# Strassen's scheme for four more K-tile pairs of a transformer block's products

## Chip, cores, metric

The kernel runs on one core of one Trainium2 chip. The metric is the device time of one launch in microseconds; lower is better.

## What is computed

One layer of a streaming encoder in float32, for 256 tokens of width 2048, with 256 memory tokens for the cross attention. All of the reference outside the four functions below only serves them (norms, rotary tables, masks, softmax):

```
h = LN(alpha*h + 0.5*SwiGLU_1(h))
h = LN(alpha*h + W_out[ sig(g_A)*(A(h) W_oA) + sig(g_B)*(B(h) W_oB) ])
      A = chunked attention with clipped relative-position bias
      B = multi-head latent attention, 16 heads of 128
h = LN(alpha*h + CrossAttn(h, LN(mem)))   (4 heads of 512)
h = LN(alpha*h + 0.5*SwiGLU_2(h))

def swiglu_ffn(x, w_in, w_out):
    g, u = jnp.split(x @ w_in, 2, axis=-1)      # x (256, 2048), w_in (2048, 2*5504)
    return (jax.nn.silu(g) * u) @ w_out
```

Three products matter here: the first SwiGLU's `x @ w_in`, the product with `w_o_b` (2048 x 2048) behind attention B, and the output projection `w_xo` (2048 x 2048) of the cross attention.

## The kernel before

**Products.** Each float32 value is split into a hi part (rounded to fp32r, by ScalarE, ACT) and a lo part (the rest, by VectorE, DVE), and a product is hi·hi + hi·lo + lo·hi, three matmul passes on TensorE (PE). The contraction runs over 16 K-tiles of 128 rows, taken in pairs, which are called steps or pairs here and numbered 0 to 7. An output group is 256 tokens (two token tiles) by two column blocks of up to 512, so four PSUM tiles. A plain pair (`mm_pair`, matmul at L300) is 2 K-tiles x 2 token tiles x 2 column blocks x 3 passes = 24 matmuls of up to 512 columns.

A Strassen pair (`mm_sums`, matmul at L354) treats the two K-tiles, two token tiles and two column blocks as a 2 x 2 product and does it with seven products (Winograd's form) instead of eight: 21 matmuls. It needs sums on both sides. Of the weights, one operation over 1024 columns (L190) and two over 512 (L192) on DVE make the summed blocks `t` in a tile called the stage; then ACT and DVE split them into hi (2 x 1024) and lo (2048). The raw weights that are split besides shrink from four blocks of 512 to three (1536). Of the activations, `sum_forms` (L306 to L323) makes four forms n5, s2, n3, s3 (one DVE operation of 512 at L310, four of 128 at L314), which are split into homes: half of a block tile, or four small `w1` tiles. Three of the seven products go to the group's own PSUM tiles `ps`, four to a second set `qs` (of the other PSUM pool); once the group's last Strassen pair is done, `shared` (L636 to L648) turns `qs` into four sums with two ACT copies and four DVE additions. Which pairs of a product are Strassen pairs is written in small tables at the top of the file (SUMS_IN, SUMS_YB, SUMS_XO), whose values are the homes of the forms. The weights are laid out for it ahead of the launch (`_pairs`).

**Order of work.** A list of items is built (`add`, `weave`), each with its weight loads, and `run` fetches raw weights through three `raw` tiles by SP's queue, splits them up to two units ahead, and emits the items. A scheduler then orders each engine's instructions by priority; the order below is what it yields. The hi tiles and the lo tiles have two buffers each.

**Places touched.** (1) The first FFN's first output group isn't in that list: `start` (L470) loads activations and weights pair by pair from the beginning of the program and does all eight pairs plainly, splitting weights in halves of 1024 (L236 lo, L235 hi). Its activations lie in blocks T0 to T3, two pairs each. After it, `ffn` (from L525) calls `hidden` for the group (SiLU times the up half) and makes the forms of pairs 2, 4 and 6 for the groups that follow. The second group's tiles are of the pool that `qs` of a first group would use. (2) Attention B's first output group, `out_b(0)` (L1140 on), uses Strassen for pairs 4 and 6; the forms are made at the end of the attention. The second group, `out_b(1)`, follows. (3) The cross attention's output (`cross`): its first two column groups go through `out_pair` with pairs 4 and 6 by Strassen, and the last head's softmax, transposition (L802) and product with the values (L1320) are woven into its first pairs; L1296 is the product of queries and keys.

## Time and profile before

| | us |
|---|---|
| median of 3 runs (2484.69 to 2485.30) | 2485.29 |
| the profiled execution | 2485.13 |
| its span in the trace | 2483.4 |
| PE busy | 2467.4 (99%) |
| DVE busy | 2066.2 (83%) |
| ACT busy | 1337.6 (54%) |

A row of the timeline gives the start in us from the span's beginning, the duration, engine, line, operation, output <- inputs, shape, and in brackets the idle time ahead of it and what ended it; rows of several instructions give the sum. In a row of the windows stand the stretch, its length, then for PE, PEld (weight loads), DVE, ACT and POOL the busy time and the number of instructions, the granted clock of PE (1.00 is full), the share of the DMA engines and GB/s. A row of PE's waits names the line that waited, the writer it waited for, the total, the count and the longest.

### The profile page before, as it was taken

To read this page: it belongs to the slowest core of one execution; us is meant where nothing else is said; L and a number is where in the kernel's file an instruction comes from. 1 tells how busy PE (TensorE), PEld (TensorE's weight loads), DVE (VectorE), ACT (ScalarE), POOL (GpSimd) and SP (SyncE) were. 2 spreads that over 40 slices of the span, in tenths; PEclk is the share of its full clock that TensorE was granted. 3 is DMA by queue.
4 is the path that set the end of the run, shared out by engine and by line. 5 is a ranking of instruction groups with operands and counts; after the bars stand their busy time and mean duration, and the time that the engine had idled before them with its cause. 6 is when DMAs were issued, how large, how long until landed. Compare 5 with 4: busy or idle time off the path is not lost.

```text
span 2483.4 us, 30482 instructions
## 1 busy us (share of the span) xinstructions
PE 2467.4 (99%) x11953; PEld 2079.9 (84%) x11953; DVE 2066.2 (83%) x2334; ACT 1337.6 (54%) x1803; POOL 31.8 (1%) x75
## 2 busy tenths in 40 slices
PE   9999999999999999999999999999999999999998
PEld 8888888889888888899888888888888888888886
DVE  6999889899778988677688798557888988898986
ACT  5555555555455555555455565545545555555552
POOL 0000000000000001000000000000000000000000
PEclk9999999999999999999999999999999999999999
DMA  7655556555645656554566547544655555655663
GB/s 259 240 196 204 187 200 211 203 187 204 237 155 210 212 203 219 178 163 141 172 235 217 189 174 248 189 155 150 209 197 187 203 187 204 210 198 202 203 216 140
DMA packets 72945, 490.16 MB, mean 197 GB/s; under 512 B 8449, under 2 KB 8961, under 8 KB 17633
## 3 DMA queue, kind: packets, MB, share of 16 engines
q1 hardware_dynamic: 67200, 468.29, 54.3%
q0 software_dynamic: 4448, 18.09, 2.2%
q8 instruction: 93, 1.52, 0.2%
q10 hardware_dynamic: 1152, 1.84, 0.2%
q14 instruction: 52, 0.42, 0.0%
HBM read 484.77 MB, written 2.10 MB: 196 GB/s over the span
## 4 chain that ended last, share of the span: by engine, by line
PE 93%; DVE 3%; DMA 2%; ACT 1%; issue 1%; DVEq 0%; ACTq 0%
PE mm L300 26%; PE at L300 24%; PE mm L354 10%; PE at L354 10%; PE mm L266 7%; PE mm L287 5%; PE mm L268 4%; PE mm L256 2%; DVE lo L246 1%; PE at L963 1%; DMA raw<-ffn_w_out_r 1%; PE at L802 1%; DMA raw<-w_xo_r 1%; PE at L1320 0%; PE at L405 0%
## 5 line engine op out<-in xcount | busy, mean ns | idle before, releaser
L243 ACT CAST hi<-raw 128x1024 fp32r<-128x1024 f32 (+1 forms) x848 | 800.9, 986 | 586.1 <-PE at L300 170.5
L246 DVE TENSOR_TENSOR lo<-raw,hi 128x2048 fp32r<-128x2048 f32 (+2 forms) x425 | 902.8, 2125 | 225.0 <-ACT hi L243 220.6
L300 PE MATMUL mm<-hi,T 128*128 128x512 f32 (+1 forms) x1280 | 298.2, 383 | 0.0
L243 ACT CAST X<-H 128x1024 fp32r<-128x1024 f32 (+1 forms) x162 | 165.0, 1034 | 220.4 <-DVE H L192 87.6
L300 PEld LDWEIGHTS mm<-hi,T 128*128 128x128 f32 x1280 | 238.3, 188 | 44.1 <-DVE H L833 0.3
L300 PE MATMUL at<-hi,T 128*128 128x512 f32 x1072 | 257.0, 389 | 0.0
L246 DVE TENSOR_TENSOR X<-H,X 128x2048 fp32r<-128x2048 f32 (+1 forms) x81 | 182.3, 2250 | 67.6 <-ACT X L243 67.6
L300 PEld LDWEIGHTS at<-hi,T 128*128 128x128 f32 x1072 | 201.1, 188 | 41.9
L300 PE MATMUL mm<-lo,T 128*128 128x512 f32 (+1 forms) x640 | 153.8, 382 | 0.0
L300 PE MATMUL at<-hi,H 128*128 128x512 f32 x592 | 140.7, 390 | 0.0
L300 PEld LDWEIGHTS mm<-lo,T 128*128 128x128 f32 x640 | 119.1, 188 | 21.8
L300 PE MATMUL at<-lo,T 128*128 128x512 f32 x536 | 132.6, 389 | 0.0
L300 PEld LDWEIGHTS at<-hi,H 128*128 128x128 f32 x592 | 110.9, 188 | 23.0 <-DVE w L647 0.2
L266 PE MATMUL mm<-T,hi 128*128 128x512 f32 x512 | 124.0, 393 | 0.0
L300 PEld LDWEIGHTS at<-lo,T 128*128 128x128 f32 x536 | 100.6, 188 | 20.9
L300 PE MATMUL mm<-hi,H 128*128 128x512 f32 x464 | 112.3, 392 | 0.0
L192 DVE TENSOR_TENSOR H<-H,raw 128x512 f32<-128x512 f32 (+1 forms) x162 | 109.3, 675 | 1.7
L266 PEld LDWEIGHTS mm<-T,hi 128*128 128x128 f32 x512 | 93.8, 188 | 19.3 <-issue 0.9
L300 PEld LDWEIGHTS mm<-hi,H 128*128 128x128 f32 x464 | 86.2, 188 | 17.6 <-DVE w L275 0.2
L190 DVE TENSOR_TENSOR H<-raw 128x1024 f32<-128x1024 f32 (+1 forms) x81 | 97.1, 1198 | 3.6 <-DMA raw<-ffn_w_in 2.4
L354 PE MATMUL mm<-X,X 128*128 128x512 f32 x348 | 95.7, 391 | 1.7 <-DVE H L236 1.7
L243 ACT CAST X<-raw 128x1024 fp32r<-128x1024 f32 (+1 forms) x54 | 55.3, 1036 | 52.1 <-DVE raw L192 31.5
(332 smaller groups left out, 3946.6 us busy)
## 6 DMA issues: line engine op xcount, KB each, us to landing
raw<-ffn_w_in SPq DMA_DIRECT2D x150, 1024.0 KB, 4.8
raw<-ffn_w_out SPq DMA_DIRECT2D x66, 1024.0 KB, 4.8
raw<-w_gate SPq DMA_DIRECT2D x32, 1024.0 KB, 4.9
raw<-ffn_w_out_r SPq DMA_DIRECT2D x16, 1024.0 KB, 4.9
raw<-w_qk SPq DMA_DIRECT2D x16, 1024.0 KB, 4.8
raw<-w_o_b SPq DMA_DIRECT2D x16, 1024.0 KB, 4.8
raw<-w_out SPq DMA_DIRECT2D x16, 1024.0 KB, 4.8
raw<-w_xk SPq DMA_DIRECT2D x16, 1024.0 KB, 5.0
```

Of the source, the lines that this page charges most:

```text
L190: self.nc.vector.tensor_tensor(two[0], two[1], raw[:, :m].unsqueeze(1).to_broadcast([P, 2, m]), ALU.add)
L192: self.nc.vector.tensor_tensor(t[:, a * m:a * m + m], t[:, b * m:b * m + m], raw[:, a * m:a * m + m], ALU.add)
L243: self.nc.scalar.copy(hi[:, c:d], src[:, c:d])
L246: self.nc.vector.tensor_tensor(lo[:, :n], src, hi[:, :n].bitcast(F32), ALU.subtract)
L256: self.nc.tensor.matmul(ps, w[wi][:, cols[j]:cols[j] + P], x.at(xi, kt), start=(j + wi + xi == 0), stop=(j == n - 1 and wi == 1),)
L266: self.nc.tensor.matmul(ps, hi[kt], x.both(kt), start=(kt == 0), stop=False)
L268: self.last_mm = self.nc.tensor.matmul(ps[:, :S], lo[kt], x.at(0, kt), start=False, stop=(kt == n - 1))
L287: self.last_mm = self.nc.tensor.matmul(ps, x.at(xi, kt)[:, tt * P:(tt + 1) * P], w[wi][:, j * 512 + c:j * 512 + c + m], start=(start and j ...
L300: self.last_mm = self.nc.tensor.matmul(ps[tt, g][:, :n], x.at(xi, kt)[:, tt * P:(tt + 1) * P], w[wi][:, c:c + n], start=first and j + wi + ...
L354: self.last_mm = self.nc.tensor.matmul(bank[:, :m], a[xi], v[wi][:, c * m:(c + 1) * m], start=own and first and wi + xi == 0, stop=own and ...
L802: self.nc.tensor.transpose(ps[:, i * P:(i + 1) * P], s[:, c:c + P], self.ident)
L963: nc.tensor.matmul(ps[:, c0:c0 + nk], q[:, tt * P:(tt + 1) * P], k[:, :nk], start=(j == 0), stop=(j == len(parts) - 1))
```

## The change

In `start`, pairs 4 and 6 go by Strassen (AT_FIRST). Their forms are made there, in the homes that the later groups use, and so no longer after `hidden`, where only pair 2's remain. The summed weights use the stage H5 and the blocks X2 and X3; `qs` comes from the pool `at`; `ffn` calls `shared` for the group ahead of `hidden`, which then takes its path with added sums. B's first output group gets pair 2 as a third Strassen pair (its forms in four `w1` tiles), and so do the cross output's first two column groups (its forms woven in at the second item). The second group of B stays as it is.

```
+AT_FIRST = 4, 6
-SUMS_YB = {4: ("T0", 0), 6: ("T0", 1)}
+SUMS_YB = {4: ("T0", 0), 6: ("T0", 1), 2: None}
+AT_YB = (2, 4, 6), (4, 6)
-SUMS_XO = {4: ("H2", 0), 6: ("H2", 1)}
+SUMS_XO = {2: None, 4: ("H2", 0), 6: ("H2", 1)}
...
+    def weight_sums(self, raw, m, t):
+        two = [v.rearrange("p (a m) -> p a m", a=2) for v in (t[:, :2 * m], raw[:, m:3 * m])]
+        self.nc.vector.tensor_tensor(two[0], two[1], raw[:, :m].unsqueeze(1).to_broadcast([P, 2, m]), ALU.add)
+        for a, b in ((2, 0), (3, 2)):
+            self.nc.vector.tensor_tensor(t[:, a * m:a * m + m], t[:, b * m:b * m + m],
+                                         raw[:, a * m:a * m + m], ALU.add)
+        return t
...
     def start(self):
...
+            if k in AT_FIRST:
+                if not qs:
+                    qs.update((a, self.group_tile(1)) for a in range(4))
+                self.forms_step(fx, SUMS_IN, k, lambda: xT, False)()
+                t4 = self.weight_sums(raw, 512, self.block("H5", (P, 2048)))
+                w = self.halves(raw[:, 512:], *self.unit()), self.halves(
+                    t4, *(self.block(g, (P, 2048), F32R) for g in SUM_HOME[0]))
+                self.mm_sums(ps, qs, w, 512, xT, fx[k], 2 * k, k == AT_FIRST[0], k == AT_FIRST[-1])
+                continue
             w = self.unit()
...
     def ffn(...)
                 if j == 0 and first is not None:
-                    main, ps = [], first
+                    main, (ps, qs, fx) = [], first
+                    self.add(lambda qs=qs: self.shared(qs, 512), prio=SOON)
...
-                    for c in SUMS_IN:
-                        self.add(self.forms_step(fx, SUMS_IN, c, xT))
+                    for c in set(SUMS_IN) - set(AT_FIRST):
+                        self.add(self.forms_step(fx, SUMS_IN, c, xT, False))
...
-            self.pair_group(g, t["w_o_b"][g], 512, KT, lambda: oB["t"], SUMS_YB, fb, ps, qs, None,
+            self.pair_group(g, t["w_o_b"][g], 512, KT, lambda: oB["t"], AT_YB[g], fb, ps, qs, None,
                             (("H5", "X2"), "X3"))
...
-        for c in SUMS_YB:
+        for c in (2, 4, 6):
             self.add(self.forms_step(fb, SUMS_YB, c, lambda: oB["t"]))
...
-        self.weave(self.collect(all_items), {2: last + [form(4)], 4: [form(6)]}, prio=0)
+        self.weave(self.collect(all_items), {1: [form(2)], 2: last + [form(4)], 4: [form(6)]}, prio=0)
```

The third argument `fresh=False` of `forms_step` lets the first form that is made, whichever it is, allocate the home's block. The weights' layout follows the tables. SP's and POOL's instructions stand in the same order as before, and PE has 12 matmuls fewer. In the changed file a line of before stands 4 lines lower up to `sum_forms` (L300 is L304, L354 is L358, L310 is L314, L246 is L250, L236 is L240) and 14 lower behind `start` (L1320 is L1334).

The scheduler's order changes in three regions, around the three places. In the start, DVE before has from pair 4 to pair 7 little but the lo parts of the weights (`lo`, in halves of 1024) and of the activations (`T`; `H_13` holds the raw activations):

```order
L236 TENSOR_TENSOR T_5_106<-H_13_126,T_5_106 128x2x256
L236 TENSOR_TENSOR lo_286<-raw_280,hi_285 128x1024 x2
L236 TENSOR_TENSOR T_6_107<-H_13_126,T_6_107 128x2x256 x2
L236 TENSOR_TENSOR lo_321<-raw_315,hi_320 128x1024 x2
L236 TENSOR_TENSOR lo_355<-raw_350,hi_354 128x1024 x2
L236 TENSOR_TENSOR lo_389<-raw_384,hi_388 128x1024 x2
L246 TENSOR_TENSOR lo_421<-raw_418,hi_420 128x2048
```

After the change it has, for pair 6 alone and what stands between (`H_49` is the stage, `w_48` the forms ahead of their split, `w_43` to `w_46` the split forms, `lo_432` belongs to pair 7, `X_53` is the lo part of the summed weights):

```order
L232 TENSOR_TENSOR H_49_392<-raw_369 128x1024
L318 TENSOR_TENSOR w_48_378<-w_47_377,w_48_378 128x128
L240 TENSOR_TENSOR w_43_373<-w_48_378,w_43_373 128x128
L240 TENSOR_TENSOR w_44_374<-w_48_378,w_44_374 128x128
L234 TENSOR_TENSOR H_49_392<-H_49_392,raw_369 128x512
L250 TENSOR_TENSOR lo_397<-raw_369,hi_396 128x1536
L240 TENSOR_TENSOR w_45_375<-w_48_378,w_45_375 128x128
L240 TENSOR_TENSOR w_46_376<-w_48_378,w_46_376 128x128
L234 TENSOR_TENSOR H_49_392<-H_49_392,raw_369 128x512
L240 TENSOR_TENSOR lo_432<-raw_427,hi_431 128x1024 x2
L250 TENSOR_TENSOR X_53_402<-H_49_392,X_52_401 128x2048
L250 TENSOR_TENSOR lo_464<-raw_461,hi_463 128x2048
```

One row of pair 6 has become the eleven ahead of the last, and the lo part of the summed weights has moved behind the lo part of pair 7. On PE, before, pair 6 is sixteen matmuls with hi and eight with lo on `T_6`, of which the first rows are:

```order
L300 MATMUL mm_121<-hi_354,T_6_107 128x512 x2
L300 MATMUL mm_122<-hi_354,T_6_107 128x512 x2
L300 MATMUL mm_123<-hi_354,T_6_107 128x512 x2
L300 MATMUL mm_124<-hi_354,T_6_107 128x512 x2
L300 MATMUL mm_121<-hi_354,T_6_107 128x512 x2
```

After, these are the last rows of pair 6 (`X_52` is the hi part of the summed weights, `at_285` to `at_288` are the tiles `qs`), with the beginning of pair 7 (`hi_431`) drawn in ahead of the products that read `X_53`:

```order
L358 MATMUL mm_122<-lo_397,w_45_375 128x512
L358 MATMUL at_285<-lo_397,T_6_107 128x512
L358 MATMUL at_286<-X_52_401,w_43_373 128x512 x2
L358 MATMUL at_288<-X_52_401,w_46_376 128x512 x2
L358 MATMUL at_287<-X_52_401,w_44_374 128x512 x2
L358 MATMUL mm_123<-X_52_401,T_6_107 128x512 x2
L304 MATMUL mm_121<-hi_431,T_6_107 128x512 x2
L304 MATMUL mm_122<-hi_431,T_6_107 128x512 x2
L358 MATMUL at_286<-X_53_402,w_43_373 128x512
L358 MATMUL at_288<-X_53_402,w_46_376 128x512
L358 MATMUL at_287<-X_53_402,w_44_374 128x512
L358 MATMUL mm_123<-X_53_402,T_6_107 128x512
```

Four matmuls of pair 7 have moved ahead of four of pair 6, which now wait for the last DVE row shown but one. At the cross output, DVE before (`lo_13462` is the lo part of pair 1, `w_2068` that of the last but one head's transposed probabilities, `sm_m` and `sm_r` the last head's softmax):

```order
L246 TENSOR_TENSOR lo_13462<-raw_13459,hi_13461 128x2048
L275 TENSOR_TENSOR w_2062_13454<-w_2062_13454,mm_13421 128x256
L236 TENSOR_TENSOR w_2068_13472<-at_13466,w_2067_13471 128x512
L790 TENSOR_REDUCE sm_m_13501<-at_13475 128x1 x2
L236 TENSOR_TENSOR H_2045_13285<-w_2062_13454,H_2045_13285 128x256
L791 TENSOR_SCALAR sm_m_13501<-sm_m_13501 128x2
L236 TENSOR_TENSOR H_2074_13516<-at_13517,H_2074_13516 128x256
L795 RECIPROCAL sm_r_13502<-sm_r_13502 128x2
```

and after (`T_2088` is the stage of pair 2's summed weights, `lo_13513` pair 1's lo part, `w_2091` the probabilities' lo part):

```order
L232 TENSOR_TENSOR T_2088_13519<-raw_13517 128x1024
L279 TENSOR_TENSOR w_2083_13505<-w_2083_13505,mm_13472 128x256
L250 TENSOR_TENSOR lo_13513<-raw_13510,hi_13512 128x2048
L804 TENSOR_REDUCE sm_m_13558<-at_13532 128x1 x2
L240 TENSOR_TENSOR H_2066_13336<-w_2083_13505,H_2066_13336 128x256
L805 TENSOR_SCALAR sm_m_13558<-sm_m_13558 128x2
L234 TENSOR_TENSOR T_2088_13519<-T_2088_13519,raw_13517 128x512
L240 TENSOR_TENSOR w_2091_13529<-at_13523,w_2090_13528 128x512
L234 TENSOR_TENSOR T_2088_13519<-T_2088_13519,raw_13517 128x512
L809 RECIPROCAL sm_r_13559<-sm_r_13559 128x2
```

The sums of pair 2's weights have moved up between the softmax's rows, and the lo part of the probabilities behind the softmax's maxima.

More of the change, by code (lines that the diff above doesn't have):

```diff
@@ L186, in form_sums @@
             if i < len(queue) and isinstance(queue[i], Sums) and i not in sums:
-                raw, m, home = fetch(i), queue[i].m, queue[i].stage
-                t = self.block(home, (P, 2048)) if home else self.raw_tile()
-                two = [v.rearrange("p (a m) -> p a m", a=2) for v in (t[:, :2 * m], raw[:, m:3 * m])]
-                self.nc.vector.tensor_tensor(two[0], two[1], raw[:, :m].unsqueeze(1).to_broadcast([P, 2, m]), ALU.add)
-                for a, b in ((2, 0), (3, 2)):
-                    self.nc.vector.tensor_tensor(t[:, a * m:a * m + m], t[:, b * m:b * m + m],
-                                                 raw[:, a * m:a * m + m], ALU.add)
-                sums[i] = t
+                raw, home = fetch(i), queue[i].stage
+                sums[i] = self.weight_sums(raw, queue[i].m, self.block(home, (P, 2048)) if home else self.raw_tile())
         def load(i):
@@ L328, in fn @@
                 tag, k = homes[c]
-                if k == 0:
+                if k == 0 and fresh or tag not in e:
                     e[tag] = self.block(tag, (P, 2, 2, 4, P), F32R)
```

10 lines of the change are left out of this document (5 added, 5 removed).

## The prediction

> **What bounds the kernel now.** I read the page first: busy times, then the granted clock.
>
> ```profile
> span 2483.4 us, 30482 instructions
> ...
> PE 2467.4 (99%) x11953; PEld 2079.9 (84%) x11953; DVE 2066.2 (83%) x2334; ACT 1337.6 (54%) x1803; POOL 31.8 (1%) x75
> ...
> PEclk9999999999999999999999999999999999999999
> ```
>
> TensorE (PE) works for 2467.4 of 2483.4 us at an undisturbed clock. So nothing but fewer or shorter matmuls can help much, and a wait of PE anywhere counts in full. VectorE (DVE), at 83%, is the only other engine near its limit. The profiled execution took 2485.13 us, 1.73 more than its span; the median of the runs shown is 2485.29. I add to 2485.13 and lift the result by 0.16 at the end.
>
> Next, the waits of PE, to see whether the engines that prepare its operands keep up:
>
> ```profile
> PE mm L354 <- DVE H L236: 1.7, 1, 1.7
> PE at L476 <- DVE w L452: 1.1, 1, 1.1
> PE at L802 <- DVE w L797: 0.6, 1, 0.6
> ```
>
> These are the three largest, and none is repeated. The kernel before feeds PE nearly without a gap.
>
> Then the chain of waits in order of time, for the price of a pair of K-tiles:
>
> ```profile
> 77.18 5.44 PE at L300 x24
> 87.38 5.44 PE at L300 x24
> ```
>
> A plain pair is 24 matmuls in 5.44 us, 0.2267 us each. Between the end of the first row (82.62) and the second (87.38) stands one Strassen pair: 4.76 us, just 21 × 0.2267. **A converted pair saves 0.68 us of PE**, if its operands come in time. The change converts four pairs: at most 2.72 us, 0.11% of the span. A measurement of this kernel can tell about 0.2% (5 us) from no change, so the size of the change sets the verdict; what remains is how much of the 2.72 survives in each place.
>
> What a Strassen pair costs is DVE work, so I need what DVE takes from one start to the next when nothing holds it:
>
> ```profile
> 16.70 1.22 DVE L236 TENSOR_TENSOR lo<-raw,hi 128x1024 fp32r<-128x1024 f32 x1
> 17.83 0.68 DVE L236 TENSOR_TENSOR T<-H,T 128x512 fp32r<-128x512 f32 x1
> ...
> 34.01 2.36 DVE L236 TENSOR_TENSOR lo<-raw,hi 128x1024 fp32r<-128x1024 f32 x2 [3.08 <-ACT hi L235]
> ...
> 48.52 1.42 DVE L192 TENSOR_TENSOR H<-H,raw 128x512 f32<-128x512 f32 x2
> ...
> 53.90 0.68 DVE L310 TENSOR_TENSOR w<-T 128x512 f32<-128x512 f32 x1
> 54.50 2.28 DVE L246 TENSOR_TENSOR X<-H,X 128x2048 fp32r<-128x2048 f32 x1
> 56.70 0.48 DVE L314 TENSOR_TENSOR w<-w 128x128 f32<-128x128 f32 x2
> ...
> 57.91 0.28 DVE L314 TENSOR_TENSOR w<-w,w 128x128 f32<-128x128 f32 x1
> 58.11 1.75 DVE L246 TENSOR_TENSOR lo<-raw,hi 128x1536 fp32r<-128x1536 f32 x1
> 59.78 0.68 DVE L236 TENSOR_TENSOR X<-w,X 128x512 fp32r<-128x512 f32 x1
> ```
>
> From start to start: 1024 wide 1.13 to 1.14, 512 wide 0.60, 2048 wide 2.20, 128 wide 0.20, 1536 wide 1.67. Each is some 0.08 below the recorded duration: the next operation starts before the record of the last ends. The row at 34.01 shows the slack before the change: in each step of the start DVE idles 3.08 us until ScalarE (ACT) has made the hi part.
>
> **The start (pairs 4 and 6 of the first group).** One row says how much room there is, and rows of PE when the room ends:
>
> ```profile
> 17.83:43.27 25.44, 25.44 (x113) 21.04 (x113) 14.39 (x15) 11.70 (x14) 0.00 (x0) 1.00 0.72 260
> ```
>
> ```profile
> 28.31 3.79 PE L300 MATMUL mm<-hi,T 128*128 128x512 f32 x16
> ...
> 50.07 3.79 PE L300 MATMUL at<-hi,T 128*128 128x512 f32 x16
> ```
>
> Pair 4 begins at 28.31 and the second group at 50.07. If PE never waited after the change, pair 4 would take 4.76 and pair 5 5.44. In the order of after, 17 matmuls of pair 6 follow (3.85) and the first four of pair 7 (0.91). Then PE wants the lo part of pair 6's summed weights, the last operand of a Strassen pair: at 28.31 + 4.76 + 5.44 + 3.85 + 0.91 = 43.27. DVE's order puts 35 operations between 17.83 and that point, where the row of the windows has 15: eight of 1024, eleven of 512, two of 1536, two of 2048 and twelve of 128. That is 8 × 1.14 + 11 × 0.60 + 2 × 1.67 + 2 × 2.20 + 12 × 0.20 = 25.86 us. **25.86 us of work stand in a gap of 25.44**: the idle time is used up. To this I add the waits inside: two operations need the result of the one ahead (0.11 each; in the row at 48.52 the second of two such operations ends after 1.42 where 0.60 + 0.68 = 1.28 would be without, so 0.14 at most), and DVE hands pair 6's forms to ACT for a cast and takes them back, 0.52 in all by my walk down the queues. ACT casts of 512 and less take up to 0.6 us (below, 1701.58), so this wait lies between nothing and 0.6. The lo part is then done at 17.84 + 25.86 + 0.74 = 44.44, and with 0.17 to reach PE (an estimate; the record's end alone is 0.08 behind the next start) its matmuls start at 44.61, not 43.27. Of this 1.34, 0.36 falls earlier: the lo of one form stands behind a 1536-wide operation on DVE and holds PE within pair 6. After 44.61 come 24 matmuls (5.44), and the second group begins at 50.05, against 50.07. **Term: 0.** The 1.36 saved is paid back in waits. Its ends: −1.36 if DVE is 1.3 us earlier, and +2.8 if each operation holds DVE for its recorded time (35 × 0.08). I take the middle because the quoted starts are unambiguous.
>
> The other new work of this group is covered. Adding up the products (two ACT copies, four DVE additions) frees the PSUM banks that the second group writes first: by the walk at 49.3 where PE wants them at 51.0. The forms that the first group now makes early are no longer made after it. The weight loads keep their order on SP's queue; with the page's 4.8 us for each they land, by the walk, at least 1.7 us before ACT needs them (pair 7 and the second group's first two are the late ones).
>
> ```profile
> raw<-ffn_w_in SPq DMA_DIRECT2D x150, 1024.0 KB, 4.8
> ```
>
> **B's first output group.** Here DVE has room.
>
> ```profile
> 1232.30 2.29 DVE L246 TENSOR_TENSOR lo<-raw,hi 128x2048 fp32r<-128x2048 f32 x1 [1.66 <-ACT hi L243]
> ```
>
> ```profile
> 1237.32 3.79 PE L300 MATMUL mm<-hi,T 128*128 128x512 f32 x16
> ```
>
> ```profile
> 1226.44:1280.00 53.56, 53.56 (x240) 44.38 (x239) 43.03 (x37) 24.55 (x27) 0.05 (x1) 1.00 0.54 189
> ```
>
> Pair 2 begins at 1237.32. Its operands need 1.14 + 2 × 0.60 (sums), 1.67 and 2.20 (two lo parts), 6.21 us, instead of 2.20: 4.0 more. The lo part of the row at 1232.30 waits 1.66 on ACT, and 10.5 us of DVE's 53.56 are idle in the stage. The walk has the first lo part ready at 1234.7 (wanted 1238.7) and the second at 1233 or shortly after (wanted 1241.2). The forms, 0.60 + 4 × 0.20 + 4 × 0.20, are made in the last attention steps, where DVE waits for ACT. **Term: −0.68**, with an end of 0 if the 4 us collide with `done` and its four multiplications; margins of 3 us and more speak against this.
>
> **The cross output.**
>
> ```profile
> 1677.34:1715.33 37.99, 37.99 (x230) 33.55 (x229) 30.77 (x54) 19.33 (x40) 0.00 (x0) 1.00 0.32 114
> ```
>
> ```profile
> 1680.64 3.22 PE L1320 MATMUL at<-w,H 128*128 128x256 f32 x24
> ```
>
> ```profile
> 1677.69 2.29 DVE L246 TENSOR_TENSOR lo<-raw,hi 128x2048 fp32r<-128x2048 f32 x1 [2.04 <-ACT hi L243]
> ...
> 1680.23 0.69 DVE L236 TENSOR_TENSOR w<-at,w 128x512 fp32r<-128x512 f32 x1
> ```
>
> ```profile
> 1699.32 2.00 ACT L243 CAST hi<-raw 128x1024 fp32r<-128x1024 f32 x2 [3.44 <-PE mm L300]
> 1701.58 0.59 ACT L235 CAST w<-at 128x512 fp32r<-128x512 f32 x1 [0.25 <-PE at L802]
> ```
>
> DVE is busy 30.77 of 37.99; the new 4.0 us and 2.2 of forms fit in the 7.2 idle us, barely. The 1024-wide sum falls into the 2.04 us of idle time ahead of the row at 1677.69. Behind it the softmax's operations and a 512-wide sum stand ahead of the lo part of the transposed probabilities (1680.23 in before): it is ready at 1683.5. PE has 13 of the first pair's matmuls (2.95) woven into the 24 that start at 1680.64, and wants it at 1683.84. A margin of 0.3. Later the cast of the last head's probabilities (before: 1701.58, in an idle ACT) stands behind the second half of a 2048-wide cast. One 1024 takes 1.0 of the 2.00 there, and that bounds the wait: 0 to 1.0. The walk gives 0.3, part of which the next matmuls would have spent anyway. **Term: −0.5**, ends −0.68 and +0.3.
>
> **Sum:** 0 − 0.68 − 0.5 = −1.2, so 2483.9 beside the profiled execution and 2484.1 beside the median; I say 2484.0. If every pair paid in full it would be 2482.4.
>
> **A rule against the change.** The rows 53.90 and 54.50 show the next DVE operation starting 0.08 before the last one's record ends. The Trainium skill, "VectorE: DVE Perf Modes", section "The DRAIN you can't avoid", says that the next operation waits until the pipeline of the last is empty. By that rule each of the start's operations would hold the engine for its whole record, and the time would be that of the second rival below; these two rows of the trace do not agree with it.
>
> **The rivals.**
> 1. *The start hides its DVE work* (chance 0.12). The lo part of pair 6 comes by 43.2. For it: ACT's hand-over may overlap with other operations, and the row at 34.01 shows 3.08 idle each step. Against it: the sum is 25.86 in 25.44 before any wait. All four pairs then pay: 2482.4.
> 2. *Slower: the start's DVE queue overruns* (0.13). The operations hold DVE for their recorded 0.28, 0.68, 1.22, 1.75 and 2.29, so 28.7 instead of 25.86 us. Pair 6's lo part is done at 47.2, the second group begins 2.8 late, and 2.8 − 0.68 − 0.5 = +1.6 gives 2486.7. It decides from 45.6 on, 1.2 us past my walk. Against it stand the starts quoted above; for it, that several of the 35 wait for results of the operation ahead or of ACT.
> 3. *The cross output gives its gain back* (0.12): the sums of weights ahead of the softmax delay the probabilities by more than the margin of 0.3, and PE waits 0.7 to 1.5: 2484.3 to 2485.1.
> 4. *The change does not do what it says* (0.03): PE's list still has all matmuls, 2485.1. The order shows 12 fewer, so only through a fault in reading it.
>
> **How the numbers follow.** My forecast (2483.3 to 2484.8) has 0.57, the rivals 0.12, 0.13, 0.12 and 0.03, and 0.03 is left for what I have not seen. The range reaches from 2482.2 (the first rival) to 2486.7: it takes in the first, third and fourth rivals and half of the second, and leaves out some 0.1. Faster by over 0.2% means below 2480.3, which no sum here reaches, 2482.4 being the floor: 0.02. Slower by over 0.2% means above 2490.3, more than twice the overrun: 0.04. The rest, 0.94, is within 0.2%.
>
> **What would show it.** PE's count falls by 12 matmuls, its busy time by 2.7. In the start, PE waits once for a DVE lo part just after the first four matmuls of pair 7 (near 43.3 to 44.6) and the second group begins near 50.05; 48.7 there is the first rival, 52 or more the second. B's first group: a pair of 4.76 at 1237 with no wait. Cross output: the pair after the third begins near 1714.8 on the scale of before plus what came earlier. The prediction is wrong if DVE's starts in the start stretch by more than 0.03 each, or if a load arrives late in the first 45 us, where the row of the windows shows the DMA queues at 0.72 and 260 GB/s.

## The result, and the profile after

The changed kernel takes **2481.99 us** (median of 22 runs, 2480.99 to 2483.89); the kernel before took 2485.61 beside it (22 runs, 2483.86 to 2488.49). The ratio is 0.9984, with a 95% interval of 0.9978 to 0.9989: some 3.6 us are gone, where 1.2 were forecast. The two profiled spans differ by 3.1 (2483.4 and 2480.3), and it is these two traces that can be compared place by place.

The page of the profile after, busy times and clock; line numbers of the helpers are 4 higher than before, those behind the start 14 higher:

```profile
span 2480.3 us, 30522 instructions
...
PE 2464.6 (99%) x11941; PEld 2076.9 (84%) x11941; DVE 2091.1 (84%) x2374; ACT 1347.4 (54%) x1821; POOL 31.8 (1%) x75
...
PEclk9999999999999999999999999999999999999999
```

PE has 12 matmuls fewer and is busy 2.8 us less: the change does what it says. The other 0.3 of the 3.1 is a balance of waits, and the list of PE's waits shows that they have changed place:

```profile
PE at L480 <- DVE w L456: 1.1, 1, 1.1
PE at L919 <- DVE X L925: 0.9, 1, 0.9
PE at L358 <- DVE X L250: 0.8, 1, 0.8
PE at L816 <- DVE w L811: 0.8, 1, 0.8
PE at L409 <- DVE h L401: 0.2, 1, 0.2
```

The largest wait of before, 1.7 at the Strassen products (L354, now L358, `mm`), is gone. Two are new. The one at L358, `at`, is the start's, which was forecast. The one at L919 stands in attention A, where the change edits nothing, and was not.

To see what each place gained I cut each trace at the same points of the program and took the time between PE's starts there (us):

| stage | before | after | difference |
|---|---|---|---|
| span's start to pair 1 of the start | 11.99 | 11.64 | −0.35 |
| **pair 1 to the second group (the start)** | 38.08 | 37.87 | −0.21 |
| second group | 42.59 | 42.41 | −0.18 |
| attention A to B's first group | 278.71 | 279.99 | **+1.28** |
| **B's first group and the next, to the transposes** | 53.04 | 52.36 | −0.68 |
| **cross output, to its pair 4** | 37.99 | 37.03 | −0.96 |
| second FFN's first Strassen pair on, one group | 44.40 | 42.70 | **−1.70** |
| from there to the end | 600.23 | 599.81 | −0.42 |

Each of the three stretches left out differs by 0.1 at most. The three places that the change edits, with the second group, give 2.0 of the 3.1. The stages in which it edits nothing give the rest: −0.35 + 1.28 − 1.70 − 0.42 = −1.2.

The rows of the start that answer to those of the prediction. PE first, from pair 4 to the second group:

```profile
27.96 0.62 PE L358 MATMUL mm<-hi,T 128*128 128x512 f32 x2
...
42.03 1.07 PE L304 MATMUL mm<-hi,T 128*128 128x512 f32 x4
43.94 0.96 PE L358 MATMUL at<-X,w 128*128 128x512 f32 x3 [0.83 <-DVE X L250]
44.74 0.39 PE L358 MATMUL mm<-X,T 128*128 128x512 f32 x1
44.97 2.89 PE L304 MATMUL mm<-hi,T 128*128 128x512 f32 x12
```

The wait stands exactly where the prediction put it, behind the first four matmuls of pair 7, and it is for the lo part of pair 6's summed weights. By the starts PE is 1.00 late there: it wanted the operand at 42.03 + 0.91 = 42.94 and began at 43.94 (the 0.83 in brackets counts from the end of the last record). The 24 matmuls behind it take 5.57 instead of 5.44. So the start loses 1.15 of its 1.36, where the prediction had 1.34. DVE says why: some of its rows of the stretch, and the row of the windows over all of it.

```profile
17.67 0.68 DVE L240 TENSOR_TENSOR T<-H,T 128x512 fp32r<-128x512 f32 x1
18.39 0.69 DVE L314 TENSOR_TENSOR w<-T 128x512 f32<-128x512 f32 x1
...
35.44 0.28 DVE L318 TENSOR_TENSOR w<-w,w 128x128 f32<-128x128 f32 x1
35.64 0.48 DVE L240 TENSOR_TENSOR w<-w,w 128x128 fp32r<-128x128 f32 x2
...
41.59 2.28 DVE L250 TENSOR_TENSOR X<-H,X 128x2048 fp32r<-128x2048 f32 x1
```

```profile
17.83:43.94 26.11, 26.04 (x36) 1.00 0.69 255
```

DVE is busy 26.04 of 26.11 us. From 17.67 to the start of the last row it takes 23.92, where the walk had 24.41. The 0.49 between them is nearly the hand-over to ACT, 0.52 in the walk: the rows at 35.44 and 35.64 follow each other without a gap, so other operations cover it. From the start of the operation behind the lo part (43.80) it takes PE 0.14 to begin; the estimate was 0.17.

In B's first group pair 2 takes 4.76, with no wait:

```profile
1237.95 0.62 PE L358 MATMUL mm<-hi,T 128*128 128x512 f32 x2
1238.40 0.62 PE L358 MATMUL mm<-hi,w 128*128 128x512 f32 x2
...
1242.71 1.52 PE L304 MATMUL mm<-hi,T 128*128 128x512 f32 x6
```

At the cross output, PE ahead of and behind the last but one head's products with the probabilities (L1320, now L1334):

```profile
1680.70 0.40 PE L1334 MATMUL at<-w,H 128*128 128x256 f32 x2
1680.94 3.14 PE L304 MATMUL mm<-hi,H 128*128 128x512 f32 x13
1683.91 2.80 PE L1334 MATMUL at<-w,H 128*128 128x256 f32 x22
1686.55 0.60 PE L816 MATMUL at<-ident,w 128*128 128x128 f32 x4
1686.90 3.12 PE L1310 MATMUL at<-X,H 128*128 128x256 f32 x24
```

and the same in before:

```profile
1683.70 0.40 PE L300 MATMUL mm<-hi,H 128*128 128x512 f32 x1
1683.94 0.68 PE L802 MATMUL at<-ident,w 128*128 128x128 f32 x4
1684.40 3.14 PE L1296 MATMUL at<-X,H 128*128 128x256 f32 x24
1687.38 3.04 PE L1320 MATMUL at<-w,H 128*128 128x256 f32 x24
1690.26 3.59 PE L300 MATMUL mm<-hi,H 128*128 128x512 f32 x15
```

In before, the 24 matmuls that began at 1680.64 (a row of the prediction) lasted until 1683.70, 3.06 us; the next 24 of the same kind take 2.88 (1687.38 to 1690.26). So 0.18 was lost there. The four transposes took 0.46 (1683.94 to 1684.40), after 0.35 (1686.55 to 1686.90), so 0.11 more was lost. After, 13 matmuls of pair 0 stand ahead of most of these products, and both losses are gone: 0.29, where the stage gained 0.28 beyond 0.68. The records of the single instructions of before fit: the third of the 24 products begins at 1680.97, just behind the end of the probabilities' lo part (1680.92), and the second transpose at 1684.07, just behind the end of the softmax's division (L797, 1684.01).

### The profile page after: what moved, and what is told of

Same layout as the page of the kernel before. It is cut to its first block, busy times and chain, and to the rows that moved or that the text cites. A ratio compares the mean times of both kernels' runs of the same rounds, so it can differ in the third digit from the quotient of the medians.

```text
span 2480.3 us, 30522 instructions
## 1 busy us (share of the span) xinstructions
PE 2464.6 (99%) x11941; PEld 2076.9 (84%) x11941; DVE 2091.1 (84%) x2374; ACT 1347.4 (54%) x1821; POOL 31.8 (1%) x75
## 4 chain that ended last, share of the span: by engine, by line
PE 95%; DVE 3%; DMA 1%; issue 0%; ACT 0%; SPq 0%; DVEq 0%; ACTq 0%
PE at L304 25%; PE mm L304 24%; PE mm L358 10%; PE at L358 10%; PE mm L291 7%; PE mm L270 7%; PE mm L272 4%; PE mm L260 2%; PE at L977 1%; PE at L291 1%; PE at L816 1%; DMA raw<-ffn_w_in 1%; PE at L1334 0%; PE at L1310 0%; PE at L1018 0%
## 5 line engine op out<-in xcount | busy, mean ns | idle before, releaser
L250 DVE TENSOR_TENSOR lo<-raw,hi 128x2048 fp32r<-128x2048 f32 (+1 forms) x427 | 905.8, 2122 | 206.7 <-ACT hi L247 204.9
L304 PE MATMUL mm<-hi,T 128*128 128x512 f32 (+1 forms) x1232 | 287.4, 382 | 0.0
L304 PEld LDWEIGHTS mm<-hi,T 128*128 128x128 f32 x1232 | 228.8, 188 | 42.9 <-ACT hi L239 0.8
L304 PE MATMUL at<-hi,T 128*128 128x512 f32 x1072 | 257.2, 389 | 0.0
L250 DVE TENSOR_TENSOR X<-H,X 128x2048 fp32r<-128x2048 f32 (+1 forms) x83 | 186.9, 2252 | 67.1 <-ACT X L247 66.0
L304 PEld LDWEIGHTS at<-hi,T 128*128 128x128 f32 x1072 | 201.1, 188 | 41.9
L304 PE MATMUL mm<-lo,T 128*128 128x512 f32 (+1 forms) x616 | 147.9, 382 | 0.0
L304 PE MATMUL at<-hi,H 128*128 128x512 f32 x592 | 140.9, 390 | 0.0
L304 PE MATMUL at<-lo,T 128*128 128x512 f32 x536 | 132.4, 389 | 0.0
L304 PEld LDWEIGHTS mm<-lo,T 128*128 128x128 f32 x616 | 114.6, 188 | 20.9
L304 PEld LDWEIGHTS at<-hi,H 128*128 128x128 f32 x592 | 110.9, 188 | 23.3 <-DVE w L661 0.4
L304 PEld LDWEIGHTS at<-lo,T 128*128 128x128 f32 x536 | 100.6, 188 | 20.9
L304 PE MATMUL mm<-hi,H 128*128 128x512 f32 x448 | 108.2, 392 | 0.0
L304 PEld LDWEIGHTS mm<-hi,H 128*128 128x128 f32 x448 | 83.4, 188 | 17.2 <-DVE w L279 0.2
L358 PE MATMUL mm<-X,X 128*128 128x512 f32 x348 | 95.7, 391 | 0.0
L358 PE MATMUL at<-X,X 128*128 128x512 f32 (+1 forms) x315 | 83.8, 384 | 0.0
```

Of the source, the lines that this page charges most:

```text
L250: self.nc.vector.tensor_tensor(lo[:, :n], src, hi[:, :n].bitcast(F32), ALU.subtract)
L304: self.last_mm = self.nc.tensor.matmul(ps[tt, g][:, :n], x.at(xi, kt)[:, tt * P:(tt + 1) * P], w[wi][:, c:c + n], start=first and j + wi + ...
L358: self.last_mm = self.nc.tensor.matmul(bank[:, :m], a[xi], v[wi][:, c * m:(c + 1) * m], start=own and first and wi + xi == 0, stop=own and ...
```

## The experiments

"Undone" means that the tables at the head of the kernel are set back. The changes in stages named below are from each run's own trace.

### Each part alone, and none

Theory 1 says that each place pays what its stage shows; theory 2 that the change shifts later loads for good, so that what was gained elsewhere comes with any part. The four kernels undo all but one part, or all three:

```
AT_FIRST = ()               # start undone, and the added `shared` under `if AT_FIRST:`
AT_YB = (4, 6), (4, 6)      # B undone, and its forms made in a loop over (4, 6)
SUMS_XO = {4: ...}          # cross output undone, and `1: [form(2)]` out of the weave
```

Only the start:

> Only the start goes by Strassen (pairs 4 and 6 of the first group); B and the cross output as before. Theory 1 (each place pays what its stage shows in the two traces): the second group begins 37.9 us after pair 1's first matmul instead of 38.1, the following group loses its 0.36 wait, so -0.4 to -0.6 us in all, with one PE wait of 0.8 to 1.0 on the lo part of pair 6's summed weights. Theory 2 (the start pays in full over many runs, the profile was unlucky): -1.3 us and no such wait. On record before: 0.

Only B's first group:

> Only B's first output group has the third Strassen pair. Both theories: pair 2 takes 4.76 instead of 5.44 us of PE with no wait beside it, -0.68 us. The stage from pair 0 of this group to the next group: 42.16 before, 41.48 here.

Only the cross output:

> Only the cross output has the third Strassen pair. Theory 1: the stage from the transposition ahead of the first pair to pair 4 takes 37.03 us as in the trace of the change, 37.99 before: -0.96, which is 0.28 more than 21 matmuls for 24; nothing else changes beyond chance. Theory 2 (the change shifts the weight loads that follow, and so takes away the 1.69 us wait at the second FFN's first Strassen pair for good): -2.6 us, that wait gone. The prediction on record: -0.5.

All undone, as a control:

> All three edits undone in the changed file (the program of before). A control: 0 us. Theory 1 (chance): of the waits of 0.9 to 1.7 us in the two traces that the edits do not touch (second FFN's first Strassen pair, attention A's key transposition, last column group), some are here, some not. Theory 2: the 1.69 us wait at the second FFN is here again.

| | median | ratio to before, interval | start | B | cross | second FFN's group | attention A |
|---|---|---|---|---|---|---|---|
| only start | 2483.92 | 0.9994, 0.9985 to 1.0003 | 37.26 | 53.05 | 37.99 | 42.71 | 279.56 |
| only B | 2484.33 | 0.9995, 0.9986 to 1.0004 | 38.08 | 52.37 | 37.99 | 44.29 | 278.67 |
| only cross | 2483.55 | 0.9993, 0.9984 to 1.0002 | 38.08 | 53.05 | 37.04 | 42.65 | 278.42 |
| none | 2485.05 | 0.9998, 0.9989 to 1.0007 | 38.08 | 53.04 | 37.99 | 43.60 | 278.60 |

(11 runs each; before in this comparison 2485.48, 33 runs.) The intervals are as wide as the parts, so the medians alone settle nothing; the stages do. B is worth −0.68 and the cross output −0.95, in each trace in which they stand, and nothing where they don't. So theory 1 holds at these two. The start is worth more alone (−0.82) than in the whole change (−0.21). And the last two columns move without an edit there: theory 1 has no account of them. Against the second theory in its plain form, the second FFN's group differs between before (44.40) and the control (43.60), which run the same work.

PE's rows of the start alone tell why the start's gain is not fixed:

```profile
43.98 0.97 PE L358 MATMUL at<-X,w 128*128 128x512 f32 x3 [0.25 <-DVE X L250]
44.78 0.39 PE L358 MATMUL mm<-X,T 128*128 128x512 f32 x1
45.01 2.89 PE L304 MATMUL mm<-hi,T 128*128 128x512 f32 x12
47.74 1.98 PE L304 MATMUL mm<-lo,T 128*128 128x512 f32 x8
49.55 2.65 PE L304 MATMUL at<-hi,T 128*128 128x512 f32 x11
```

Here PE began pair 1 at 12.29, 0.65 later than in the whole change (11.64), and yet the lo part is used at the same time (43.98 and 43.94) and the second group begins at the same time (49.55 and 49.51). **Before, PE paced the start** (38.08 in every trace without the edit, wherever it began); **now DVE does.** In the four traces with both pairs and this order, DVE takes 23.91 to 23.93 from the row that stands at 17.67 in after to the start of that lo part, wherever PE began. What PE saves is eaten by a wait when PE begins early, and kept when it begins late. When it begins is chance: the five traces that have the start of before and 12 warm-up matmuls have pair 1 at 11.54 to 12.26.

### What moved in the stages that nothing edits

The second FFN's first Strassen pair waited 1.69 in before. DVE began its sums late, since a 1 MB load had not landed:

```profile
1829.27 1.23 DVE L190 TENSOR_TENSOR H<-raw 128x1024 f32<-128x1024 f32 x1 [2.42 <-DMA raw<-ffn_w_in]
```

After, the same operation waits less:

```profile
1826.59 1.23 DVE L232 TENSOR_TENSOR H<-raw 128x1024 f32<-128x1024 f32 x1 [1.38 <-DMA raw<-ffn_w_in]
```

The DMA rows give that load's time: before (issued in the window 1823.2 to 1823.4), the control (1822.2 to 1823.0), and after (1821.6 to 1821.9).

```profile
raw<-ffn_w_in SPq DMA_DIRECT2D x1, 1024.0 KB, 6.0
```

```profile
raw<-ffn_w_in SPq DMA_DIRECT2D x1, 1024.0 KB, 5.9
```

```profile
raw<-ffn_w_in SPq DMA_DIRECT2D x1, 1024.0 KB, 4.9
```

What lies beside it? In before, in the window 1826.3 to 1826.5, the page's otherwise idle queue q8 moves one packet of 0.02 MB:

```profile
q8 instruction: 1, 0.02, 29.7%
```

After, its packet at this place comes in 1825.6 to 1825.9, behind the issue by 4.16 instead of 3.19:

```profile
q8 instruction: 1, 0.02, 18.5%
```

The page has the whole queue:

```profile
q8 instruction: 93, 1.52, 0.2%
```

93 packets of 16 KB for some 23,900 instructions of PE (matmuls and weight loads) are one for each 256; that they fetch PE's instructions is worked out from this count and from the queue's name. **Theory F**: such a fetch, when it falls into the first 3.7 us of a 1 MB load, delays it by about 1 us. An edit that takes out PE instructions moves all later fetches against the loads. **Theory C**: what differs in the unedited stages is chance from run to run. Since the number of PE instructions ahead of a place sets which one brings the fetch, the length of the warm-up (matmuls that compute nothing) is a handle that edits nothing else:

```
- WARM = 12
+ WARM = 8          # all parts undone
```

> The three edits undone, and 8 instead of 12 warm-up matmuls at the program's beginning: 16 PE instructions (8 matmuls, 8 weight loads) fewer, nothing else. Theory F (a 16 KB fetch of PE instructions, one for about 256 of them, delays a weight load by about 1 us when it falls into the load's first 3.7 us): the fetch near 1825 comes 1.8 us later, 4.9 instead of 3.1 us after the issue of the load of the second FFN's first Strassen pair; that load lands in 4.8 to 5.0 instead of 5.9 us, and the stage of the second FFN's first group takes 42.7 instead of 43.6 to 44.4: -0.9 to -1.7 there, and other places may win or lose by their own fetches. Theory C (chance): the stage takes 43.6 to 44.4 as in the three traces that have neither the new start nor the new cross output.

```
- WARM = 12
+ WARM = 15         # the whole change
```

> The change with 15 instead of 12 warm-up matmuls: 12 PE instructions more. Theory F: the fetch near 1825 comes 1.4 us earlier, about 2.7 instead of 4.1 us after the load's issue; the load takes 5.9 to 6.0 instead of 4.95 us, PE waits 0.9 to 1.7 us for the first Strassen pair's sums, and the second FFN's first group takes 43.6 to 44.4 instead of 42.7. Theory C: 42.7, as in the trace of the change.

```
- WARM = 12
+ WARM = 22         # all parts undone
```

> The three edits undone, and 22 warm-up matmuls: 40 PE instructions more. Theory F: the fetch near 1825 comes 4.5 us earlier, more than 1 us ahead of the load's issue, so the load lands in about 4.8 and the second FFN's first group takes 42.7, the same as with 16 instructions fewer. A theory by which more PE instructions only make it worse: 43.6 to 44.4 or more. The first pairs begin up to 2 us later, since the warm-up itself is longer.

With 8 and all undone: 2484.94 (11 runs, ratio 0.9993, 0.9984 to 1.0002). With 15 and the change: 2482.09 (11 runs, 0.9981, 0.9972 to 0.9989). With 22 and all undone, a single run: 2489.1, beside 2486.14 (27 runs) for before in the three. With all parts undone, the load of the second FFN takes 5.02 with 8 and 4.81 with 22, where the control with 12 had 5.91 and its fetch 3.12 behind the issue; now the fetch is 4.16 behind, and ahead of the issue. So the load's time follows the fetch. But several numbers missed:

- With 8, the fetch moved by 1.0 us, not 1.8, and the group took 43.38, not 42.7, because another wait stood there: a vector loaded from `gb` on POOL's queue, issued some 1.5 us behind two 1 MB loads, came late and held DVE for 0.59. Before has 0.61 of this wait and the control, with the same work, none; so this part is chance, and theory C is right for it. The two parts can be told apart over all 13 traces: PE's wait is nothing in the six with neither, 0.52 to 0.79 in the four with the `gb` wait alone, 0.94 in the control, which has the late load alone, and 1.69 and 1.59 in before and only B, which have both. So some 0.9 of the 1.69 belongs to the load.
- With 15, the fetch near 1825 didn't move (4.0 behind the load), and PE's 0.52 wait there goes with a `gb` wait of 0.37.
- With 8 and with 22 the second group begins 1 to 1.5 us later (51.11 and 51.55, before 50.07), so a changed warm-up costs in the start what it was to show later. The single 2489.1 says nothing on theory F.

With 15 another place, attention A, came out as theory F has it. In the changed kernel attention A loses 1.3. There two 1 MB loads are issued one after the other; in after the fetch falls 0.8 behind the second one's issue, and that load takes 8.0:

```profile
raw<-w_qk SPq DMA_DIRECT2D x1, 1024.0 KB, 8.0
```

```profile
971.41 0.44 PE L919 MATMUL at<-ident,H 128*128 128x128 f32 x2 [0.90 <-DVE X L925]
```

In before the second load takes 4.8 (issued in 956.1 to 956.6), and the first, which has the fetch 3.6 behind its issue, 6.1. PE doesn't wait:

```profile
raw<-w_qk SPq DMA_DIRECT2D x1, 1024.0 KB, 4.8
```

```profile
971.09 0.44 PE L905 MATMUL at<-ident,H 128*128 128x128 f32 x2
```

The second load is late by 3 us in after, not by the 1 us of theory F.

With 15, the fetch is back behind the first load (3.13) and the stage takes 278.55, where after took 279.99 and before 278.71.

### The handle by itself: twelve PE instructions more

```
+ for _ in range(3):
+     nc.tensor.matmul(warm[:, :16], self.ones, self.ones[:, :16], start=True, stop=True)
```

Three matmuls of 16 columns at the end of the warm-up, 12 of PE's instructions (each matmul here is two, with a weight load each), with the whole change. Pair 1 begins at 12.76 in this trace, in after at 11.64, so the count is not all that differs.

> The change and three matmuls of 16 columns behind the warm-up: 12 PE instructions more at nearly no time. Theory F: the fetch near 955 moves from 0.8 us behind the issue of one load of w_qk to some 3 us behind the one ahead of it; the load that took 7.6 to 8.0 us takes 4.8 again, the wait of 0.5 to 0.9 us at attention A's transposition goes, and the stage from attention A to B's output takes 278.6 instead of 279.3 to 280.0: the total falls by 0.5 to 0.9, to about 2481.3. Theory C (chance): stage and total as in the change.

Measured: 2481.42 (11 runs, 0.9983, 0.9974 to 0.9991; before here 2485.66, 27 runs). In attention A the second load takes 5.1 and there is no wait at L919 (L921 in this kernel):

```profile
raw<-w_qk SPq DMA_DIRECT2D x1, 1024.0 KB, 5.1
```

The stage takes 278.60, as expected. But the fetch moved by less than expected: it is 0.39 behind the second load's issue instead of 0.8, and not some 1.2 ahead of it. The wait went all the same. By the times this kernel and the change can't be told apart (0.9983 and 0.9984).

One trace is a hint only. Sorted by the number of PE instructions that run ahead of a place, against before (a matmul less is two, with its weight load), the 13 traces leave little to chance:

| place | PE instructions ahead | traces | the load, us |
|---|---|---|---|
| attention A, second load | 12 or 16 fewer | 4 | 7.5 to 8.0 |
| | 6 fewer, as many, or 40 more | 9 | 4.7 to 5.2 |
| second FFN's first Strassen pair | as many or 6 fewer | 4 | 5.9 to 6.0 in three, 4.9 in only cross |
| | 12 to 24 fewer, or 40 more | 9 | 4.8 to 5.0 |
| last 1 MB load of `ffn_w_out_r` | as many or 6 fewer | 4 | 5.5 to 6.1 |
| | 12 to 24 fewer, or 40 more | 9 | 4.7 to 5.1 |

In attention A the four with the late load take 279.3 to 280.0 for the stage and the nine others 278.4 to 278.7; the four are after, only start, the order of the next section, and the control with 8 warm-up matmuls, which has none of the edits. So the instruction count is the handle. The arithmetic from a count to a fetch's time is not understood: two kernels with the same count can differ by more than 1 us in it.

All traces together bear theory F out as well. I took from all 13 every 1 MB load of SP's queue that had no other transfer under way at its issue and none issued in the 3 us behind it, and sorted them by the time from its issue to the next packet of q8:

| fetch behind the load's issue, us | loads | median us to landing |
|---|---|---|
| none within 5 | 2091 | 4.79 |
| 0 to 0.6 | 34 | 5.13 |
| 0.6 to 1 | 25 | 5.29 |
| 1 to 2 | 18 | 5.64 |
| 2 to 3 | 9 | 5.91 |
| 3 to 3.7 | 13 | 5.98 |
| 3.7 to 4.2 | 140 | 4.77 |
| 4.2 to 5 | 213 | 4.82 |

Of the 65 loads between 0.6 and 3.7, 46 took over 5.5 us; of the 2091 without a fetch, two did.

The records of the single packets show what is late. Each of these loads ends with 16 packets of 4 bytes, as many as there are DMA engines. Where no fetch falls, the last of the 16 comes 0.06 behind the one before it (median); where one falls within 0.6 to 3.7, 0.76. For the second FFN's load, before has 15 of them at 1827.23 to 1827.90 and the last at 1828.79, and the fetch's own packet takes 0.95. So it is one sixteenth of the load that comes late, by about the time of the fetch's packet; that it is the share of the engine that carried the fetch is worked out from this, since the records don't name the engine. In attention A it is one of 16 too, but 3.0 late (15 by 959.98, the last at 962.98).

The last 1 MB load of `ffn_w_out_r`, in the tail, is a third case: with its fetch within 0.9 to 3.6 it took 5.5 in before and 5.7 to 6.1 in the control, only B and only the cross output, with a wait of PE of 0.3 to 0.9. In eight of the other traces, after among them, the fetch came later than 4.2 and the load took 4.7 to 5.1, with no wait. That is most of the −0.42 of the last stage.

### How much the start is worth

The lo part that PE waits for, moved ahead of that of pair 7 on DVE:

```
+ lo_sums = nc.vector.tensor_tensor(lo4, t4, hi4.bitcast(F32), ALU.subtract)
...
+ with self.tc.issue_after(lo_sums.ins) if k == 7 else nullcontext():
      nc.vector.tensor_tensor(w[1][...], ..., ALU.subtract)   # pair 7's lo part
```

> The change, with the start's order altered in one point: DVE makes the lo part of pair 6's summed weights ahead of the lo part of pair 7 instead of behind it. If the start is paced by DVE up to that operation (theory 1): the wait there goes (it had been 0.25 to 0.83), the second group begins 36.8 to 37.1 us after pair 1's first matmul, 1 us sooner than 37.87, and the total falls by 0.3 to 1.0. If the wait's place is taken by another (pair 7's lo part, or ACT), 37.3 or more and no gain.

Measured: 2482.74 (11 runs, 0.9986, 0.9977 to 0.9995; before 2486.14); the start took 37.55, within the 37.24 to 37.87 of the four traces with the order as it was. DVE's and PE's rows:

```profile
40.83 2.29 DVE L515 TENSOR_TENSOR X<-H,X 128x2048 fp32r<-128x2048 f32 x1 [1.11 <-ACT X L514]
```

```profile
43.18 0.96 PE L358 MATMUL at<-X,w 128*128 128x512 f32 x3 [0.53 <-DVE X L515]
43.98 0.39 PE L358 MATMUL mm<-X,T 128*128 128x512 f32 x1
44.21 3.80 PE L304 MATMUL mm<-hi,T 128*128 128x512 f32 x16
```

The lo part begins only 0.76 earlier, since DVE now waits 1.11 for ACT's hi part of the sums; and PE has lost the four matmuls of pair 7 that stood ahead, so, counted from pair 1, it wants the operand 0.9 sooner. A wait for ACT has taken the place of the one for DVE's queue.

Only the first of the start's two pairs:

```
- AT_FIRST = 4, 6
+ AT_FIRST = 4,
```

> The change with only pair 4 of the start by Strassen, 3 matmuls more than the change. Theory 1: DVE has 9.1 us less to do ahead of pair 7, so no PE wait for the lo part of summed weights; 37.40 us from pair 1 to the second group (38.08 - 0.68), against 37.26 to 37.87 with both pairs. The second pair of the start was then worth 0.1 us on average instead of 0.68. If DVE is not what paces the start, 38.08 - 0.3 = 37.8 or so. Total within 0.5 us of the change's, lower if attention A's wait goes with 6 PE instructions more.

The change without its start:

> The change without its start (B's first group and the cross output alone, 6 matmuls fewer than before). Theory 1 with F: the start's own gain is lost (38.08 us from pair 1 to the second group instead of 37.3 to 37.9, and 42.6 instead of 42.4 for that group), about +0.7; but the 12 PE instructions that the start saved are back, so the fetch near 955 comes 3.1 to 3.6 us after a load's issue as in the four traces without the new start, and attention A's wait of 0.5 to 0.9 is gone: in all about the time of the change, 2481.7 to 2482.6 where before has 2485.5. If the start paid its 1.36 in full, 1 us more than the change.

| | median (11 runs) | ratio, interval | span | start | attention A |
|---|---|---|---|---|---|
| only pair 4 at the start | **2480.74** | 0.9980, 0.9971 to 0.9989 | 2478.1 | 37.40 | 278.65 |
| no pair at the start | 2481.25 | 0.9983, 0.9974 to 0.9992 | 2480.3 | 38.08 | 278.59 |
| both, and 12 PE instructions more | 2481.42 | 0.9983, 0.9974 to 0.9991 | 2480.0 | 37.24 | 278.60 |

(All with the other two parts; before 2485.66.) Without a pair at the start the time is below what was expected (2481.7 to 2482.6), and the fetch is 4.0 behind the first load of attention A, not 3.1 to 3.6; the wait there is gone as expected. With pair 4 alone PE never waits in the start:

```profile
38.14 3.79 PE L304 MATMUL mm<-hi,T 128*128 128x512 f32 x16
41.77 1.98 PE L304 MATMUL mm<-lo,T 128*128 128x512 f32 x8
43.58 3.79 PE L304 MATMUL mm<-hi,T 128*128 128x512 f32 x16
47.21 1.98 PE L304 MATMUL mm<-lo,T 128*128 128x512 f32 x8
49.02 3.33 PE L304 MATMUL at<-hi,T 128*128 128x512 f32 x14
```

38.08 − 37.40 = 0.68: one pair in full. The four traces with both pairs and this order have 37.87, 37.26, 37.48 and 37.24, 37.46 on the mean: the second pair adds nothing. Where PE begins alike (pair 1 at 11.62 with pair 4 alone, at 11.64 in after), it costs 0.5. **Only pair 4 is the fastest of all kernels here, below both before and the change as it is**; that it beats the change is seen in its trace (the start without a wait, and none in attention A), and by medians of different comparisons (0.9980 and 0.9984, with intervals that overlap), so only its lead over before is settled by times. It also has the late load of attention A out of the way (the second load takes 5.2). Of the 2.2 that its trace is shorter than after's, attention A is 1.3 and the start 0.5; the first follows from its count of instructions and not from the start's work.

## Why the prediction was wrong, step by step

**What bounds the kernel.** Right: 12 matmuls fewer, 2.8 us less of PE, and four pairs as the largest direct gain. The change is within 0.2%, as forecast (3.62 of 2485.61 is 0.15%), but the time lies 0.2 us below the range's lower end. Two things failed: the sum gave every stage outside the edited places nothing, without a reason, and there the trace moved by −1.2; and the cross output's term of −0.5 was too small by 0.5.

**The start: term 0, measured −0.2 (−0.8 where PE begins later).** The mechanism and the place were right: the idle time of DVE is used up, and one wait stands behind the first four matmuls of pair 7. The size failed in "DVE hands pair 6's forms to ACT for a cast and takes them back, 0.52 in all by my walk": no time at all went there (DVE took 23.92 where the walk had 24.41). It was bounded by nothing and 0.6, and the lower end was true. A second thing I didn't see: I reckoned everything from pair 4 at 28.31, as if PE's beginning were fixed. Over the traces with a warm-up of 12 or 15, PE began pair 1 anywhere from 11.5 to 12.8, and when DVE paces the start, the gain depends on it. The second group is 0.18 shorter besides in this trace, for which I had no term (42.40 to 42.44 in four of the six traces with the new start, 42.6 in those without); the forms that the later groups use are made earlier. That this is the reason was not tried.

**B's first group: −0.68, measured −0.68.** The margins of 3 us held.

**The cross output: −0.5, measured −0.96.** "It is ready at 1683.5 … and PE wants it at 1683.84, a margin of 0.3" was right in its size: the probabilities' lo part ends at 1683.63 by DVE's row (1682.94, 0.69), and the products that can use it begin at 1683.91.

```profile
1682.94 0.69 DVE L240 TENSOR_TENSOR w<-at,w 128x512 fp32r<-128x512 f32 x1
```

What failed is the other step, the cast of the last head's probabilities that was to cost 0.2 net. The cast did come late as the walk had it: it begins 0.92 behind the transposes ahead of it, in before 0.64. But PE had five other matmuls to do meanwhile (in before four), so the delay costs nothing that can be seen. And I set −0.68 as the end of the term, without asking what the stage lost before: the row that I quoted, 24 matmuls in 3.22, held 0.18 of wait, and the transposes 0.11 more. The matmuls that the new order puts ahead cover both. That the 0.18 was a wait for the lo part (ended 1680.92 in before, where the products began at 1680.64) is read from those rows and records and was not tried by itself.

**The sum.** The edited places gave −2.0 with the second group, not −1.2. The other −1.2 of the trace's 3.1 came from stages that I took as fixed. "2482.4 being the floor" was the wrong sentence: it counted PE's work that goes away, but not the waits of before. Of these, some 0.9 of the 1.69 in the second FFN and the 0.3 in the tail depended on when a packet of instructions falls, and the rest of the 1.69 on when a `gb` vector lands. The change has moved such packets for better (the second FFN, the tail) and for worse (attention A). Part of it is not the change's at all: the control has 0.8 less than before in the second FFN's group with the same work.

**The rivals.** The first (all four pairs pay) came nearest in time, for a wrong reason: the start didn't pay in full. The second, slower by an overrun, is refuted: with each operation holding DVE for its recorded time, the operations up to pair 6's lo part would have taken 28.7; they took 26.2 (17.67 to 43.87), most of them starting 0.08 before the record of the last ends. The Trainium skill's page "VectorE: DVE Perf Modes", section "The DRAIN you can't avoid", which the prediction set against the change, says besides that a next operation which is not held starts earlier; the prediction left this out, and these starts agree with it. The third (the cross output gives its gain back) did not come, though its margin was really as thin as 0.3. The fourth is out by the count of matmuls.

**What stays open.** Why the late sixteenth of a load is 3 us late in attention A and 1 us elsewhere; and how the fetch's time follows from the count of instructions: the fetch was to move by 1.8, 1.4, 4.5 and some 2 us with 8, 15 and 22 warm-up matmuls and with the 12 instructions, and moved by 1.0, 0.2, 6.0 and 0.4. And differences below 1 us between the kernels are within the intervals of the times; they rest on single traces, in which other waits come and go (PE at L409 waits 0.2 in after and 1.1 with 12 PE instructions more).

## What to carry to other kernels

In a kernel with one engine at 99%, read what each stage loses *before* the change, in the very rows that carry your terms, before you call the removed work the floor: a reordering may cover a wait that was already there. When a change makes the second engine the pacer of a stage, convert until its idle time is gone and no further; here the first pair paid in full and the second nothing. And when the sum of the terms is a few us, time stages and not kernels: unedited stages moved by more than the edit was worth.

## What the runs showed of the hardware

A queue q8 moves 93 packets of 16 KB, one for about 256 of PE's 23,906 matmuls and weight loads, and a packet takes some 0.96 us (median of the 13 traces). One that comes 0.6 to 3.7 us behind the issue of a 1 MB load goes with a landing after 5.69 instead of 4.79 us by the medians (65 and 2091 loads), and it is one of the load's 16 closing packets that is late. So taking out six matmuls can move a wait of 0.3 to 0.9 us in or out far behind the edit. A 256 KB load behind two of 1 MB is uncertain as well: the `gb` vector ahead of the second FFN landed 4.7 to 6.3 us after its issue over the 13 traces, and held DVE for up to 1.0.
